# The tail of a two-layer decoder trunk on one core: the last 512 columns in two halves, the scaling ahead of the root, the last store on another queue

## The chip, the core and the metric

The kernel runs on one core of a Trainium2 chip. The core has five engines that run side by side, each with its own queue of instructions: TensorE (PE in the profile) multiplies matrices into PSUM, VectorE (DVE) and ScalarE (ACT) work elementwise on PSUM and SBUF, GpSimd (POOL) does little here, and SyncE (SP) issues most transfers. ACT can issue transfers too. PSUM has eight banks; a tile of 128 partitions by 512 float32 fills one. The metric is the device time of one execution in microseconds, lower is better.

## The reference

Two decoder layers on 256 tokens (16 learned tokens are put ahead and dropped at the end) with model width 1024. Each layer is a half-step SwiGLU block, a mixer (causal pooling in layer 0, differential attention in layer 1), and a second half-step SwiGLU block. Only the end of the last SwiGLU block matters here:

```python
def rmsnorm(x, g):
    xf = x.astype(jnp.float32)
    y = xf * lax.rsqrt(jnp.mean(xf * xf, axis=-1, keepdims=True) + EPS)
    return (y * g.astype(jnp.float32)).astype(x.dtype)

def swiglu(h, w1, w3, w2):
    return (jax.nn.silu(h @ w1) * (h @ w3)) @ w2
...
        f = swiglu(rmsnorm(h, ffn_norm_pre[i, 1]), ffn_w1[i, 1], ffn_w3[i, 1], ffn_w2[i, 1])
        h = h + 0.5 * rmsnorm(f, ffn_norm_post[i, 1])
    return h[:, N_META:]
```

So for each token: the 1024 columns of `f` are summed as squares, the inverse root of their mean scales them, the vector `ffn_norm_post` (the post-norm's) scales them by column, and half of that is added to `h`.

## The kernel before

Activations lie transposed (width on the partitions) until the last block's second projection, whose result has the tokens on the partitions. Every float32 product is three passes: each operand is split into a high and a low part, and `mm3` issues high x high, low x high and high x low into the same accumulation. Weights come in units of 128 x 1024 through SP's queue and are split by ACT (high) and DVE (low).

The order of the instructions on PE, ACT, DVE and SP is the order in which the code is written (`manual_schedule`); the framework only adds the waits on semaphores. A wait for another engine stands on the instruction that needs it, and everything behind that instruction on the same engine waits too.

`last_ffn` is the last SwiGLU block, without the 16 learned tokens. `ys[t][d]` are four PSUM banks: `t` is the block of 128 tokens, `d` the half of the 1024 output columns. `down(b)` adds the hidden block `b` to all four. The last three hidden blocks are kept back (`last`) and added bank by bank at the end, so that the banks become final one after the other: nine matmuls for each. When a bank is final,

- ACT squares it with `accum_out`, which leaves the sum over its columns in one column of `ms`;
- DVE makes `yg`, the bank times 0.5 times `gp` (the post-norm's vector, the same on all partitions);
- after the first bank DVE adds epsilon to the first sum (`part`); after the second, ACT takes the inverse root of the whole (`r`), DVE forms `v`, and with `q` and again `r` does one Newton step on the root;
- DVE makes `o`, `yg` times `r` plus `hn[t]` (the residual, transposed back earlier), in pieces of 512, 256 and 256 columns, and each piece is stored as soon as it is there. All stores are issued by SP but the middle one of the last token block, which ACT issues.

Of the kernel before, what the change touches and what calls it, by code (L numbers as in the profile page):

```python
# [9 lines left out]
F32 = mybir.dt.float32  # L10
F32R = mybir.dt.float32r
AF = mybir.ActivationFunctionType
ALU = mybir.AluOpType
# [3 lines left out]
P = 128  # L17
# [6 lines left out]
NB = FF // P  # L24
# [151 lines left out]
def trunk(ctx, tc, ht, w13a, w13b, w2t, w2n, wqkva, wqkv, wo, wp, lamv, mask, band, gpost, out):  # L176
    nc = tc.nc
# [68 lines left out]
    pfirst = const.tile([P, 2 * NK], F32, name="pfirst")  # L246
    pbg = const.tile([P, NK], F32, name="pbg")

    def mm3(out_ap, a, b, start, stop):

        nc.tensor.matmul(out_ap, lhsT=a[0], rhs=b[0], start=start, stop=False)  # L251
        nc.tensor.matmul(out_ap, lhsT=a[1], rhs=b[0], start=False, stop=False)  # L252
        nc.tensor.matmul(out_ap, lhsT=a[0], rhs=b[1], start=False, stop=stop)  # L253

    def wcol(parts, c, n=P):
        return parts[0][:, c:c + n], parts[1][:, c:c + n]

    def xcol(x, lo, hi):
        return x[0][:, lo:hi], x[1][:, lo:hi]
# [20 lines left out]
    def rsqrt(s, n, eps, tag, width=L, ahead=None):  # L280

        y = rsqrt_table(s, n, eps, tag, width)
        if ahead is not None:
            table(ahead, y[:, 0:1])
        newton(y, y, s, n, -0.5 * EPS if eps else 0.0)
        return y

    def table(func, src):

        nc.scalar.activation(out=dummy, in_=src, func=func)  # L290
# [218 lines left out]
    def first_blocks(res, us, spans, sums, refill, order):  # L509

        taken = []

        def go(k, pairs, start=False, stop=False):

            while len(taken) <= (6 * k + 5) // 8:
                taken.append(w.take())
            for a, x in pairs:
                for q, n in enumerate(spans):
                    u, c = divmod(6 * k + q, 8)
                    nc.tensor.matmul(us[q][:, :n], lhsT=taken[u][a][:, c * P:(c + 1) * P], rhs=x[:, :n],  # L520
                                     start=start, stop=stop)
                start = False

        res.lead = order[0]
        res.begin()
        ahead = sum(x is not None for x in res.hi)
        for k in range(ahead):
            go(k, [(0, res.hi[k]), (1, res.hi[k])], start=k == 0)
            if k == EXACT[res.n] and res.post.near:
                res.post.exact()  # L530
                res.refine()
        for i, k in enumerate(order):
            last = i == NK - 1
            res.tile(k, None if last else order[i + 1])
            hi, lo = res.x[k]
            if k >= ahead:
                go(k, [(0, hi)], start=k == 0)
                if last:
                    sums()
                go(k, [(1, hi)])  # L540
            elif last:
                sums()
            go(k, [(0, lo)], stop=last)
            left = 6 if last else 6 * min(order[i + 1:]) // 8
            w.refill(refill[i], held=max(SLACK, len(taken) - left))
# [570 lines left out]
    def last_ffn(res, fp, ubank, ybank, epsb):  # L1116
        n = SEQ

        us = [ubank() for _ in range(3)] + [ybank() for _ in range(3)]
        s2 = ybank()  # L1120

        def sums():
            nc.tensor.matmul(s2[:, :n], lhsT=ones, rhs=res.acc[:, :n], start=True, stop=True)
            for t in range(2):
                nc.tensor.matmul(s2[:, 300 + t:301 + t], lhsT=res.acc[:, t * P:(t + 1) * P], rhs=ones[:, 0:1],
                                 start=True, stop=True)

        first_blocks(res, us, [n] * 6, sums, REFILL, ORDER[4])
        r2 = rsqrt(s2[:, :n], n, True, "r2", ahead=AF.Silu)
        nc.vector.tensor_scalar(epsb, s2[:, 300:302], -0.5 * EPS, -2.0 * EPS, ALU.add, ALU.mult)  # L1130
        gate = Gate(n, r2, fp, False)
        gate.group(us)
        gate.paired = True
        gs = gate.parts
        gp = fp.tile([P, D], F32, name="gp")
        nc.sync.dma_start(out=gp, in_=gpost)
        hn = [fp.tile([P, D], F32, name=f"hn{t}", tag=f"hn{t}") for t in range(2)]

        def down(b):
            parts = w.take()  # L1140
            g = gs.pop(b)
            for t in range(2):
                for d in range(2):
                    mm3(ys[t][d], xcol(g, t * P, (t + 1) * P), wcol(parts, d * 512, 512), b == 0, b == NB - 1)

        for b in range(3, NB):
            u1, u3 = ubank(), ubank()
            for c, u in enumerate((u1, u3)):
                parts = w.take()
                for k in range(NK):  # L1150
                    nc.tensor.matmul(u, lhsT=parts[0][:, k * P:(k + 1) * P], rhs=res.pairs[k], start=k == 0, stop=k == NK - 1)  # L1151
                for k in range(NK):
                    nc.tensor.matmul(u[:, :n], lhsT=parts[1][:, k * P:(k + 1) * P], rhs=res.x[k][0], start=False,  # L1153
                                     stop=k == NK - 1, skip_group_check=True)
                if c == 0:
                    s = gate.silu(gate.scale(u1))
                    w.refill(2)
                else:
                    gate.product(b, s, u3)
                    w.refill(1)  # L1160
                    gate.low()
            if b == 3:
                ys = [[ybank(), ybank()] for _ in range(2)]
            down(b - 3)
            w.refill(1)
            if b in (8, 10, 12, 14):
                t, d = divmod((b - 8) // 2, 2)
                tr = ubank()
                for q in range(4):
                    nc.tensor.transpose(tr[:, q * P:(q + 1) * P], h[4 * d + q][:, t * P:(t + 1) * P], ident)  # L1170
                nc.scalar.copy(out=hn[t][:, d * 512:(d + 1) * 512], in_=tr)
        table(AF.Abs_reciprocal_sqrt, gate.s[:, 0:1])
        last = [(w.take(), gs.pop(b)) for b in range(NB - 3, NB)]
        for t in range(2):
            ms = fp.tile([P, 2], F32, tag="ms", name="ms", bufs=2)
            yg = fp.tile([P, D], F32, tag="yg", name="yg", bufs=2)
            junk = fp.tile([P, 512], F32, tag="junk", name="junk", bufs=1)
            o = fp.tile([P, D], F32, tag="o", name="o", bufs=2)
            for d in range(2):
                y = ys[t][d]  # L1180
                for q, (parts, g) in enumerate(last):
                    mm3(y, xcol(g, t * P, (t + 1) * P), wcol(parts, d * 512, 512), False, q == 2)
                nc.scalar.activation(out=junk, in_=y, func=AF.Square, scale=1.0 / 32.0, accum_out=ms[:, d:d + 1])
                if d == 0:
                    part = fp.tile([P, 1], F32, tag="part", name="part", bufs=2)
                    nc.vector.tensor_tensor(part, ms[:, 0:1], epsb[:, t:t + 1], ALU.add)
                else:
                    v = fp.tile([P, 1], F32, tag="v", name="v", bufs=2)
                    r = fp.tile([P, 1], F32, tag="r", name="r", bufs=2)
                    q = fp.tile([P, 1], F32, tag="q", name="q", bufs=2)  # L1190
                    nc.scalar.activation(out=r, in_=ms[:, 1:2], func=AF.Abs_reciprocal_sqrt, bias=part)
                    nc.vector.tensor_scalar(v, ms[:, 1:2], part, -0.5, ALU.add, ALU.mult)
                c = slice(d * 512, (d + 1) * 512)
                nc.vector.scalar_tensor_tensor(yg[:, c], y, 0.5, gp[:, c], ALU.mult, ALU.mult)
            nc.vector.scalar_tensor_tensor(q, r, r, v, ALU.mult, ALU.mult)
            nc.vector.scalar_tensor_tensor(r, q, 1.5, r, ALU.add, ALU.mult)
            for q, (c0, c1) in enumerate(((0, 512), (512, 768), (768, 1024))):
                nc.vector.scalar_tensor_tensor(o[:, c0:c1], yg[:, c0:c1], r, hn[t][:, c0:c1], ALU.mult, ALU.add)
                (nc.scalar if t and q == 1 else nc.sync).dma_start(out=out[t, :, c0:c1], in_=o[:, c0:c1])


    mp0, mp1 = C_MPOST, C_MPOST + NK
# [32 lines left out]
    with ExitStack() as stack:  # L1235
# [7 lines left out]
        with tc.tile_pool(name="ffn3", bufs=1, reuse_waits="tile") as fp:  # L1243

            epsb = fp.tile([P, 56], F32, name="epsb")[:, 0:2]
# [77 lines left out]
```

## Time and profile before

| what | value |
|---|---|
| median of 3 runs | 953.18 us (953.13 to 954.76) |
| the profiled execution | 953.05 us |
| its span, first to last instruction | 951.3 us |
| PE busy | 938.2 us (99%) |
| DVE, ACT busy | 636.8 us (67%), 502.4 us (53%) |
| mean granted TensorE clock | 0.998 of full speed |
| last matmul ends | at 944.53 us of the span |
| last store issued | at 948.08 us |

The span runs from the first to the last instruction; the time of the execution has 1.75 us more around it. Positions in the trace are microseconds from the start of the span. A matmul's start is recorded and its end modelled, and neighbouring matmuls overlap in the records, so the distance of two starts is what one costs. Rows of the timeline give start, duration, engine (PEld is the load of the stationary operand, SPq and ACTq are issues of transfers), line, operation, what is written <- what is read, shape, and in brackets the idle time before it with what ended it.

### The profile page before, as it was taken

To read this page: it belongs to the slowest core of one execution; us is meant where nothing else is said; L and a number is where in the kernel's file an instruction comes from. 1 tells how busy PE (TensorE), PEld (TensorE's weight loads), DVE (VectorE), ACT (ScalarE), POOL (GpSimd) and SP (SyncE) were. 2 spreads that over 40 slices of the span, in tenths; PEclk is the share of its full clock that TensorE was granted. 3 is DMA by queue.
4 is the path that set the end of the run, shared out by engine and by line. 5 is a ranking of instruction groups with operands and counts; after the bars stand their busy time and mean duration, and the time that the engine had idled before them with its cause. 6 is when DMAs were issued, how large, how long until landed. Compare 5 with 4: busy or idle time off the path is not lost.

```text
span 951.3 us, 17449 instructions
## 1 busy us (share of the span) xinstructions
PE 938.2 (99%) x6945; PEld 901.6 (95%) x6945; DVE 636.8 (67%) x1092; ACT 502.4 (53%) x865; POOL 15.4 (2%) x24
## 2 busy tenths in 40 slices
PE   9999999999999999999999999999999999999997
PEld 9999999998999999999999999999998998888885
DVE  7955554458975555448855554468877899777774
ACT  7744444435654445545744455446766756445432
POOL 0000000210000000000000000000001000000000
PEclk9999999999999999999999999999999999999999
DMA  9755557730475556551755556532523628655521
GB/s 318 266 197 177 168 156 220 221 117 1 143 257 176 170 155 199 176 190 45 265 179 178 166 172 188 186 99 91 177 95 121 206 89 294 215 190 184 180 89 44
DMA packets 48321, 160.74 MB, mean 169 GB/s; under 512 B 5360, under 2 KB 8944, under 8 KB 48240
## 3 DMA queue, kind: packets, MB, share of 16 engines
q1 hardware_dynamic: 47952, 159.31, 52.1%
q8 instruction: 54, 0.88, 0.4%
q10 hardware_dynamic: 288, 0.33, 0.1%
q14 instruction: 27, 0.22, 0.1%
HBM read 158.57 MB, written 1.05 MB: 168 GB/s over the span
## 4 chain that ended last, share of the span: by engine, by line
PE 95%; DVE 3%; ACT 1%; issue 1%; DMA 0%; DVEq 0%; ACTq 0%
PE bank L253 23%; PE bank L252 23%; PE bank L251 23%; PE bank L520 8%; PE bank L1151 7%; PE bank L1153 4%; PE bank L688 1%; DVE wlo L145 1%; PE bank L641 1%; PE bank L653 1%; PE bank L642 1%; DMA raw<-in_w13a 0%; ACT sc L875 0%; PE bank L852 0%; PE bank L843 0%
## 5 line engine op out<-in xcount | busy, mean ns | idle before, releaser
L145 DVE TENSOR_TENSOR wlo<-raw,whi 128x1024 fp32r<-128x1024 f32 (+1 forms) x296 | 353.7, 1198 | 58.5 <-PE bank L252 26.9
L133 ACT CAST whi<-raw 128x1024 fp32r<-128x1024 f32 (+1 forms) x296 | 299.8, 1029 | 50.7 <-PE bank L253 45.9
L251 PE MATMUL bank<-x,whi 128*128 128x272 f32 (+1 forms) x752 | 217.3, 289 | 0.0
L253 PE MATMUL bank<-x,whi 128*128 128x272 f32 (+1 forms) x752 | 216.8, 288 | 0.0
L252 PE MATMUL bank<-x,wlo 128*128 128x272 f32 (+1 forms) x752 | 215.7, 287 | 0.2 <-DVE wlo L145 0.2
L252 PEld LDWEIGHTS bank<-x,wlo 128*128 128x128 f32 x752 | 141.3, 188 | 0.5 <-DVE wlo L145 0.4
L251 PEld LDWEIGHTS bank<-x,whi 128*128 128x128 f32 x752 | 141.3, 188 | 0.5 <-issue 0.4
L253 PEld LDWEIGHTS bank<-x,whi 128*128 128x128 f32 x752 | 141.6, 188 | 0.0
L252 PE MATMUL bank<-ghi,wlo 128*128 128x272 f32 x484 | 140.0, 289 | 0.0
L251 PE MATMUL bank<-ghi,whi 128*128 128x272 f32 x484 | 140.0, 289 | 0.0
L253 PE MATMUL bank<-glo,whi 128*128 128x272 f32 x484 | 140.0, 289 | 0.0
L571 ACT ACTIVATE ua<-ua 128x272 f32<-128x272 f32 (+1 forms) x88 | 37.1, 429 | 142.6 <-DVE ua L557 142.6
L580 ACT CAST ghi<-ua 128x272 fp32r<-128x272 f32 (+1 forms) x88 | 36.1, 417 | 112.0 <-DVE ua L577 112.0
L251 PEld LDWEIGHTS bank<-ghi,whi 128*128 128x128 f32 x484 | 91.9, 190 | 0.0
L253 PEld LDWEIGHTS bank<-glo,whi 128*128 128x128 f32 x484 | 91.2, 188 | 0.0
L252 PEld LDWEIGHTS bank<-ghi,wlo 128*128 128x128 f32 x484 | 90.9, 188 | 0.0
L253 PE MATMUL bank<-xlo,whi 128*128 128x272 f32 x304 | 87.8, 289 | 0.0
L251 PE MATMUL bank<-xhi,whi 128*128 128x272 f32 x304 | 87.4, 287 | 0.0
L252 PE MATMUL bank<-xhi,wlo 128*128 128x272 f32 x304 | 87.3, 287 | 0.0
L577 DVE TENSOR_TENSOR ua<-bank,ua 128x272 f32<-128x272 f32 (+1 forms) x69 | 29.5, 438 | 71.4 <-PE bank L253 71.4
L1151 PE MATMUL bank<-xp,whi 128*128 128x512 f32 x304 | 76.1, 392 | 0.0
L1151 PEld LDWEIGHTS bank<-xp,whi 128*128 128x128 f32 x304 | 55.5, 188 | 10.5
(243 smaller groups left out, 1371.4 us busy)
## 6 DMA issues: line engine op xcount, KB each, us to landing
raw<-in_w13b SPq DMA_DIRECT2D x152, 512.0 KB, 4.2
raw<-in_w2t SPq DMA_DIRECT2D x48, 448.0 KB, 3.4
raw<-in_w2t SPq DMA_DIRECT2D x24, 512.0 KB, 3.6
raw<-in_w2n SPq DMA_DIRECT2D x22, 512.0 KB, 3.7
raw<-in_w13a SPq DMA_DIRECT2D x18, 512.0 KB, 4.3
raw<-in_wqkv SPq DMA_DIRECT2D x18, 512.0 KB, 4.2
raw<-in_wo SPq DMA_DIRECT2D x8, 512.0 KB, 3.7
raw<-in_wqkva SPq DMA_DIRECT2D x6, 512.0 KB, 4.2
```

The lines of the kernel that those rows point to most:

```text
L133: self.nc.scalar.copy(out=hi[:, :n], in_=self.raws[u][:, :n])
L145: self.nc.vector.tensor_tensor(lo[:, :n], raw[:, :n], hi[:, :n].bitcast(F32), ALU.subtract)
L251: nc.tensor.matmul(out_ap, lhsT=a[0], rhs=b[0], start=start, stop=False)
L252: nc.tensor.matmul(out_ap, lhsT=a[1], rhs=b[0], start=False, stop=False)
L253: nc.tensor.matmul(out_ap, lhsT=a[0], rhs=b[1], start=False, stop=stop)
L520: nc.tensor.matmul(us[q][:, :n], lhsT=taken[u][a][:, c * P:(c + 1) * P], rhs=x[:, :n], start=start, stop=stop)
L571: nc.scalar.activation(out=a[:, :self.n], in_=a[:, :self.n], func=AF.Silu)
L577: nc.vector.tensor_tensor(s[:, :n], self.sum(u3), s[:, :n], ALU.mult)
L580: nc.scalar.copy(out=hi, in_=s[:, :n])
L641: nc.tensor.matmul(y[:, :n], lhsT=a[0], rhs=x[0], start=b == 0, stop=False)
L1151: nc.tensor.matmul(u, lhsT=parts[0][:, k * P:(k + 1) * P], rhs=res.pairs[k], start=k == 0, stop=k == NK - 1)
L1153: nc.tensor.matmul(u[:, :n], lhsT=parts[1][:, k * P:(k + 1) * P], rhs=res.x[k][0], start=False, stop=k == NK - 1, skip_group_check=True)
```

## The change

For the last token block (`t` = 1) the second bank is no longer accumulated by nine matmuls of 512 columns. Nine matmuls make its columns 0 to 255 final, then nine its columns 256 to 511; both halves stay in the one bank. Each half has its own Square, its own column of `ms` and its own `yg`. The first token block keeps two pieces of 512.

For both token blocks `yg` now stands ahead of `part`, and the last `yg` ahead of `v`, `q` and `r` (the small tiles are all named `n` now: `part`, `v`, `r` and `q2`). The last store of the last token block is issued by ACT and the middle one by SP, the other way round than before.

The new argument `part` of `mm3` and the place of `stop` in `down` only set flags of the accumulation groups.

```diff
--- before.py
+++ after.py
@@ -246,11 +246,11 @@
     pfirst = const.tile([P, 2 * NK], F32, name="pfirst")
     pbg = const.tile([P, NK], F32, name="pbg")
 
-    def mm3(out_ap, a, b, start, stop):
-
-        nc.tensor.matmul(out_ap, lhsT=a[0], rhs=b[0], start=start, stop=False)
-        nc.tensor.matmul(out_ap, lhsT=a[1], rhs=b[0], start=False, stop=False)
-        nc.tensor.matmul(out_ap, lhsT=a[0], rhs=b[1], start=False, stop=stop)
+    def mm3(out_ap, a, b, start, stop, part=False):
+
+        nc.tensor.matmul(out_ap, lhsT=a[0], rhs=b[0], start=start, stop=False, skip_group_check=part)
+        nc.tensor.matmul(out_ap, lhsT=a[1], rhs=b[0], start=False, stop=False, skip_group_check=part)
+        nc.tensor.matmul(out_ap, lhsT=a[0], rhs=b[1], start=False, stop=stop, skip_group_check=part)
 
     def wcol(parts, c, n=P):
         return parts[0][:, c:c + n], parts[1][:, c:c + n]
@@ -1141,7 +1141,7 @@
             g = gs.pop(b)
             for t in range(2):
                 for d in range(2):
-                    mm3(ys[t][d], xcol(g, t * P, (t + 1) * P), wcol(parts, d * 512, 512), b == 0, b == NB - 1)
+                    mm3(ys[t][d], xcol(g, t * P, (t + 1) * P), wcol(parts, d * 512, 512), b == 0, b == NB - 4 and t == d == 1)
 
         for b in range(3, NB):
             u1, u3 = ubank(), ubank()
@@ -1172,31 +1172,31 @@
         table(AF.Abs_reciprocal_sqrt, gate.s[:, 0:1])
         last = [(w.take(), gs.pop(b)) for b in range(NB - 3, NB)]
         for t in range(2):
-            ms = fp.tile([P, 2], F32, tag="ms", name="ms", bufs=2)
+
+            cuts = (0, 512, 768, 1024) if t else (0, 512, 1024)
+            m = len(cuts) - 1
+            ms = fp.tile([P, m], F32, tag=f"ms{t}", name="ms")
             yg = fp.tile([P, D], F32, tag="yg", name="yg", bufs=2)
             junk = fp.tile([P, 512], F32, tag="junk", name="junk", bufs=1)
             o = fp.tile([P, D], F32, tag="o", name="o", bufs=2)
-            for d in range(2):
-                y = ys[t][d]
+            part, v, r, q2 = [fp.tile([P, 1], F32, tag=f"n{i}", name="n", bufs=2) for i in range(4)]
+            for i in range(m):
+                c = slice(cuts[i], cuts[i + 1])
+                n = cuts[i + 1] - cuts[i]
+                y = ys[t][cuts[i] // 512][:, cuts[i] % 512:cuts[i] % 512 + n]
                 for q, (parts, g) in enumerate(last):
-                    mm3(y, xcol(g, t * P, (t + 1) * P), wcol(parts, d * 512, 512), False, q == 2)
-                nc.scalar.activation(out=junk, in_=y, func=AF.Square, scale=1.0 / 32.0, accum_out=ms[:, d:d + 1])
-                if d == 0:
-                    part = fp.tile([P, 1], F32, tag="part", name="part", bufs=2)
-                    nc.vector.tensor_tensor(part, ms[:, 0:1], epsb[:, t:t + 1], ALU.add)
-                else:
-                    v = fp.tile([P, 1], F32, tag="v", name="v", bufs=2)
-                    r = fp.tile([P, 1], F32, tag="r", name="r", bufs=2)
-                    q = fp.tile([P, 1], F32, tag="q", name="q", bufs=2)
-                    nc.scalar.activation(out=r, in_=ms[:, 1:2], func=AF.Abs_reciprocal_sqrt, bias=part)
-                    nc.vector.tensor_scalar(v, ms[:, 1:2], part, -0.5, ALU.add, ALU.mult)
-                c = slice(d * 512, (d + 1) * 512)
+                    mm3(y, xcol(g, t * P, (t + 1) * P), wcol(parts, cuts[i], n), False, q == 2, n < 512)
+                nc.scalar.activation(out=junk[:, :n], in_=y, func=AF.Square, scale=1.0 / 32.0, accum_out=ms[:, i:i + 1])
                 nc.vector.scalar_tensor_tensor(yg[:, c], y, 0.5, gp[:, c], ALU.mult, ALU.mult)
-            nc.vector.scalar_tensor_tensor(q, r, r, v, ALU.mult, ALU.mult)
-            nc.vector.scalar_tensor_tensor(r, q, 1.5, r, ALU.add, ALU.mult)
+                if i < m - 1:
+                    nc.vector.tensor_tensor(part, ms[:, i:i + 1], part if i else epsb[:, t:t + 1], ALU.add)
+            nc.scalar.activation(out=r, in_=ms[:, m - 1:m], func=AF.Abs_reciprocal_sqrt, bias=part)
+            nc.vector.tensor_scalar(v, ms[:, m - 1:m], part, -0.5, ALU.add, ALU.mult)
+            nc.vector.scalar_tensor_tensor(q2, r, r, v, ALU.mult, ALU.mult)
+            nc.vector.scalar_tensor_tensor(r, q2, 1.5, r, ALU.add, ALU.mult)
             for q, (c0, c1) in enumerate(((0, 512), (512, 768), (768, 1024))):
                 nc.vector.scalar_tensor_tensor(o[:, c0:c1], yg[:, c0:c1], r, hn[t][:, c0:c1], ALU.mult, ALU.add)
-                (nc.scalar if t and q == 1 else nc.sync).dma_start(out=out[t, :, c0:c1], in_=o[:, c0:c1])
+                (nc.scalar if t and q == 2 else nc.sync).dma_start(out=out[t, :, c0:c1], in_=o[:, c0:c1])
 
 
     mp0, mp1 = C_MPOST, C_MPOST + NK
```

How it stands on the engines at the end of the program, with the waits. On PE, the end before (bank_9757 is `ys[1][1]`; `whi`, `wlo` are the weights' parts, `ghi`, `glo` the hidden block's):

```order
L253 MATMUL bank_9756<-wlo_11069,ghi_11126 128x512
L251 MATMUL bank_9757<-whi_10999,ghi_10996 128x512
L252 MATMUL bank_9757<-whi_10999,glo_10997 128x512
...
L252 MATMUL bank_9757<-whi_11043,glo_11127 128x512
L253 MATMUL bank_9757<-wlo_11069,ghi_11126 128x512
```

and now, around the seam between the halves:

```order
L253 MATMUL bank_9756<-wlo_11069,ghi_11126 128x512
L251 MATMUL bank_9757<-whi_10999,ghi_10996 128x256
...
L252 MATMUL bank_9757<-whi_11043,glo_11127 128x256
L253 MATMUL bank_9757<-wlo_11069,ghi_11126 128x256
L251 MATMUL bank_9757<-whi_10999,ghi_10996 128x256 [waits DVE_49]
L252 MATMUL bank_9757<-whi_10999,glo_10997 128x256
```

Nine matmuls became eighteen into the same bank, and the first of the second half waits for a count of DVE's that is reached by `yg` of the first half.

On DVE, the last token block before (bank_9756 is `ys[1][0]`):

```order
L1186 TENSOR_TENSOR part_11198<-ms_11184,epsb_9368 128x1 [waits Activation_49]
L1194 SCALAR_TENSOR_TENSOR yg_11185<-bank_9756,gp_9686 128x512
L1192 TENSOR_SCALAR v_11211<-ms_11184,part_11198 128x1 [waits DVE_49,Activation_49]
L1194 SCALAR_TENSOR_TENSOR yg_11185<-bank_9757,gp_9686 128x512
L1195 SCALAR_TENSOR_TENSOR q_11213<-r_11212,v_11211 128x1 [waits DVE_49,Activation_49]
L1196 SCALAR_TENSOR_TENSOR r_11212<-q_11213,r_11212 128x1 [waits DVE_49]
```

and now (n_11188 is `part`, n_11189 `v`, n_11190 `r`, n_11191 `q2`):

```order
L1190 SCALAR_TENSOR_TENSOR yg_11185<-bank_9756,gp_9686 128x512 [waits Activation_49]
L1192 TENSOR_TENSOR n_11188<-ms_11184,epsb_9368 128x1
L1190 SCALAR_TENSOR_TENSOR yg_11185<-bank_9757,gp_9686 128x256 [waits Activation_49]
L1192 TENSOR_TENSOR n_11188<-ms_11184,n_11188 128x1 [waits DVE_49]
L1190 SCALAR_TENSOR_TENSOR yg_11185<-bank_9757,gp_9686 128x256 [waits Activation_49]
L1194 TENSOR_SCALAR n_11189<-ms_11184,n_11188 128x1 [waits DVE_49]
L1195 SCALAR_TENSOR_TENSOR n_11191<-n_11190,n_11189 128x1 [waits DVE_49,Activation_49]
L1196 SCALAR_TENSOR_TENSOR n_11190<-n_11191,n_11190 128x1 [waits DVE_49]
```

The last `yg` moved ahead of `v`, each `yg` waits for the Square of the same bank, and one `yg` and one `part` are new.

On ACT, the last token block before:

```order
L1183 ACTIVATE junk_11186,ms_11184<-bank_9756 128x512 [waits PE_49]
L1183 ACTIVATE junk_11186,ms_11184<-bank_9757 128x512 [waits PE_49,Activation_49]
L1191 ACTIVATE r_11212<-ms_11184,part_11198 128x1 [waits DVE_49,Activation_49]
L1199 DMA out_0<-o_11187 128x256 [waits DVE_49]
L1318 UNCONDITIONAL_BRANCH
```

and now:

```order
L1189 ACTIVATE junk_11186,ms_11184<-bank_9756 128x512 [waits PE_49]
L1189 ACTIVATE junk_11186,ms_11184<-bank_9757 128x256 [waits PE_49,Activation_49]
L1189 ACTIVATE junk_11186,ms_11184<-bank_9757 128x256 [waits DVE_49,PE_49]
L1193 ACTIVATE n_11190<-ms_11184,n_11188 128x1 [waits DVE_49,Activation_49]
L1199 DMA out_0<-o_11187 128x256 [waits DVE_49]
```

The Square of the second half waits for DVE as well as for PE. The store at the end is the middle piece before, the last piece now.

## The prediction

> **What bounds the kernel now.** I read the page's first part, then the chain that ended last for the final microseconds, then the timeline of the same stretch.
>
> ```profile
> span 951.3 us, 17449 instructions
> PE 938.2 (99%) x6945; PEld 901.6 (95%) x6945; DVE 636.8 (67%) x1092; ACT 502.4 (53%) x865; POOL 15.4 (2%) x24
> ```
>
> TensorE is busy 99% of the span, so the whole kernel is bound by matmuls; the change leaves all of them but the last nine alone. What it can move is the tail behind them. The chain there (start, length, what):
>
> ```profile
> 944.29 0.24 PE bank L253
> ...
> 944.62 0.07 ACT junk L1183
> ...
> 945.11 0.20 ACT junk L1183
> ...
> 945.34 0.21 DVE v L1192
> ...
> 945.61 0.46 issue
> 946.07 0.22 DVE q L1195
> ...
> 946.31 0.17 DVE r L1196
> ...
> 946.50 0.75 DVE o L1198
> 947.26 0.40 DVEq L1318
> 947.65 0.40 DVE o L1198
> ```
>
> The last matmul ends at 944.53, and 6.8 us remain to 951.3: sum of squares on ACT (0.7 us), root and Newton step (1.2), three products on DVE (1.55), then the last store. Even a perfect overlap could touch only the first two, and 0.2% of 953.18 us, about what a measurement of this kernel can tell from no change, is 1.91 us.
>
> The timeline rows of the tail (start, duration):
>
> ```profile
> 941.39 0.68 DVE L1194 SCALAR_TENSOR_TENSOR yg<-bank,gp 128x512 f32<-128x512 f32 x1
> 941.99 0.21 DVE L1195 SCALAR_TENSOR_TENSOR q<-r,v 128x1 f32<-128x1 f32 x1
> 942.32 0.39 PE L251 MATMUL bank<-whi,ghi 128*128 128x512 f32 x1
> 942.43 1.54 DVE L1198 SCALAR_TENSOR_TENSOR o<-yg,r,hn 128x512 f32<-128x512 f32 x3
> 943.01 0.19 ACT L1183 ACTIVATION_READ_ACCUMULATOR junk<-bank 128x1 f32 x1
> 943.89 0.15 DVE L1186 TENSOR_TENSOR part<-ms,epsb 128x1 f32<-128x1 f32 x1
> 943.96 0.68 DVE L1194 SCALAR_TENSOR_TENSOR yg<-bank,gp 128x512 f32<-128x512 f32 x1
> 944.13 0.39 PE L253 MATMUL bank<-wlo,ghi 128*128 128x512 f32 x1
> 944.62 0.60 ACT L1183 ACTIVATE junk<-bank 128x512 f32<-128x512 f32 x1 [1.41 <-PE bank L253]
> 945.34 0.29 ACT L1191 ACTIVATE r<-ms,part 128x1 f32<-128x1 f32 x1
> 945.47 0.68 DVE L1194 SCALAR_TENSOR_TENSOR yg<-bank,gp 128x512 f32<-128x512 f32 x1
> ```
>
> See three things. The nine matmuls that the change halves start at 942.32 and the ninth at 944.13, (944.13 - 942.32) / 8 = 0.226 us apart, without a gap. DVE is occupied with the first token block's products until 942.43 + 1.54 = 943.97, so it is late for the second block: the accumulator of that block's first 512 columns was read at 943.01 + 0.19 = 943.20, yet `part` came at 943.89. And `r` was ready at 945.34 + 0.29 = 945.63, yet `q` started at 946.07, because `yg` (started 945.47) stood between; one `yg` keeps DVE 941.99 - 941.39 = 0.60 us.
>
> **The change, part by part.**
>
> *The halves.* Nine matmuls of 512 columns become nine on columns 512-767 and nine on columns 768-1023, both in one PSUM bank. In the built program the tenth of them waits for a DVE count, and ACT's Square of the second half waits for DVE too: these stand in the order shown with the change. That count is reached by `yg` of the first half, which itself waits for the first half's Square. So PE stops after nine, until ACT and then DVE have read the first half. Before, nothing stood between. Behind the waiting matmul on PE are only the other eight; waiting for them are Square, `yg`, the root and all that follows.
>
> Where the trace shows PE write a bank while another engine reads it, there would be a row for what overlap costs; it shows none, since each bank is read after its ninth matmul.
> The Trainium skill, page "PSUM — Partial Sum Buffer", section "PSUM bank collisions raise a hardware error", says that any two of TensorE, ScalarE and VectorE collide when they access one bank on the same partitions at once, disjoint columns and two readers included, and that guards go by bank, not by address. By that rule the wait cannot be removed while both halves share a bank, and the sum is the loss below; by dependences on columns alone it would be the small gain of the first rival. No run here shows a collision.
>
> Prices for 256 columns, from the attention block:
>
> ```profile
> 755.66 0.39 ACT L449 ACTIVATE sq<-bank 128x256 f32<-128x256 f32 x1
> 729.40 0.42 DVE L272 SCALAR_TENSOR_TENSOR nt<-bank,nt 128x256 f32<-128x256 f32 x1
> 730.40 0.48 DVE L932 SCALAR_TENSOR_TENSOR of<-bank,subg,oy 128x256 f32<-128x256 f32 x1
> 729.61 0.39 PE L251 MATMUL bank<-ohi,whi 128*128 128x256 f32 x1 [0.84 <-ACT am L902]
> 729.84 0.28 PE L252 MATMUL bank<-ohi,wlo 128*128 128x256 f32 x1
> 730.53 0.28 PE L252 MATMUL bank<-ohi,wlo 128*128 128x256 f32 x1
> ```
>
> Matmuls of 256 columns follow each other at (730.53 - 729.84) / 6 = 0.115 us (six steps between these two rows), and the first after a wait needs 0.23 until the second. A Square of 256 takes 0.39 against 0.60, 0.21 less. A `yg` of 256 takes 0.42 to 0.48; I take 0.42, whose row has the same kind of operands (a bank and a full tile), 0.26 less than 0.68, so it keeps DVE 0.34.
>
> What a restart of PE after DVE costs, from the longest such wait of the trace:
>
> ```profile
> 228.22 0.44 DVE L310 TENSOR_TENSOR x<-a,rt 128x272 fp32r<-128x272 f32 x1
> 228.78 0.80 PEld L520 LDWEIGHTS bank<-x,whi 128*128 128x128 f32 x6 [2.09 <-issue]
> 228.81 1.00 PE L520 MATMUL bank<-x,whi 128*128 128x272 f32 x6 [1.69 <-DVE x L310]
> ```
>
> DVE ended at 228.66, PE started at 228.81: 0.15 us.
>
> *Scaling ahead of the root.* `yg` now stands before `v` on DVE. In the first token block this makes `v` and `q` later: `yg` starts at about 941.26, `v` at 941.86, `q` at 941.86 + 0.21 + 0.02 = 942.09 instead of 941.99, so the three products end at 944.07 instead of 943.97. That 0.10 us is passed on, since DVE is the late one in the next block.
>
> The second block, step by step:
> - First half, PE: 942.32 + 8 x 0.115 = 943.24, last one ends at +0.28 = 943.52. Square starts 0.1 later (944.62 against 944.53 before), at 943.62, its sum is read by about 944.1.
> - DVE: `yg` of the first 512 columns starts at 943.97 + 0.10 - 0.08 (`part` began 0.08 before the products' end) = 943.99; `part` 0.60 later, 944.59; `yg` of the first half 0.07 later (943.96 - 943.89), 944.66, and ends at 945.08. Here DVE, not ACT, is last.
> - PE restarts at 945.08 + 0.15 = 945.23, after 945.23 - 943.52 = 1.7 us of standing still. The ninth starts 0.23 + 7 x 0.115 = 1.04 later and ends at 946.27 + 0.28 = 946.55. Before it was 944.53: 2.0 us later.
> - Square of the second half at 946.64. From Square to the first instruction that uses its sum were 945.34 - 944.62 = 0.72; less 0.21 is 0.51: 947.15. `yg` 0.34, `v` 0.21 + 0.02, then `q` at 947.72. Before, that stretch was 946.07 - 945.34 = 0.73, now 0.57: the move ahead of the root and the shorter half together give 0.16 back, the shorter Square 0.21.
> - `q` to `o` as before (946.50 - 946.07 = 0.43): the products start at 948.15 instead of 946.50, 1.65 us later.
>
> *The last store.* The middle store goes from ACT's queue to SP's, the last from SP's to ACT's.
>
> ```profile
> 947.69 0.36 ACTq L1199 DMA_DIRECT2D out<-o  x1
> 948.08 0.33 SPq L1199 DMA_DIRECT2D out<-o  x1
> ...
> out<-o ACTq DMA_DIRECT2D x1, 128.0 KB, 2.2
> out<-o SPq DMA_DIRECT2D x1, 128.0 KB, 2.3
> ```
>
> (The last two rows are of the answer on transfers: queue, KB, us to landing.) DVE's last product ended at 948.05 and SP issued 0.03 later: SP had been free, so no wait is taken away. SP gets the middle store one issue (0.33) after its first, which is done before the product is ready. Landing took 2.2 on ACT's queue and 2.3 on SP's: worth -0.1 to 0, and between the ends I take -0.05, as the two transfers also share what they move with. The range keeps 0.15 either way.
>
> *The rest* (flags of the matmul groups, names of the small tiles, one more `part` of 0.15 us beside PE's standstill) adds nothing to the path; the instructions ahead are the same. If that `part` lost its cover, it would cost 0.15.
>
> Sum: +1.65 - 0.05 = +1.6 us. The profiled execution (953.05 us, span 951.3, 1.75 around it) becomes 954.65; it stood 0.13 under the median of the runs, so the forecast is 953.18 + 1.6 = **954.8 us**, +0.17%: a loss, but inside what counts as no change.
>
> **Rivals.**
> 1. *The halves do overlap*: PE goes on at 943.47 as if the wait were met. For it: ACT is idle and could take the first half. Against it: the wait in the built order, and DVE's backlog. Then PE ends at 944.55 as before, and the 0.21 and 0.16 are won: -0.4 with the store, 952.8 us, still no change. Nothing in 6.8 us of tail gives the 1.91 for "faster".
> 2. *The clock falls during the standstill* (slower by more than 0.2%). The granted clock (next-to-last columns: PEclk, DMA share, GB/s):
>
> ```profile
> 227.00:229.00 2.00, 0.31 (x2) 0.22 (x2) 1.90 (x5) 1.75 (x4) 0.00 (x0) 1.00 0.00 0
> ...
> 947.00:947.50 0.50, 0.00 (x0) 0.00 (x0) 0.50 (x2) 0.00 (x0) 0.00 (x0) 0.72 0.00 0
> 947.50:948.00 0.50, 0.00 (x0) 0.00 (x0) 0.50 (x2) 0.00 (x0) 0.00 (x0) 0.50 0.00 0
> ```
>
> After the last matmul the clock halves: 0.72 over half a microsecond, at 1.0 and 0.5, puts the step at 947.22, 2.7 us after 944.53. Against the rival: 1.69 us without a matmul at 227-229 left it at 1.00, and 1.7 is what I expect now. For it: one sample of each. Nine matmuls at half the rate cost about 1.0 to 1.3 more, 955.9 us; a fall with three of the nine to come (+0.3) is the point from which it decides.
> The Trainium skill, page "TensorE: Matmul & The Clock Gate", section "What's actually happening", has the gate judge free-running windows of about 3.4 us; by that, half a window of standstill should not close it, but where the window lies varies from run to run.
>
> **How the numbers follow.** The waiting case has 0.80, with a range of its own of 954.3 to 955.3: `yg` at 0.48 adds 0.1 twice, the store 0.15, the restart and the two hand-overs of ACT some 0.1 each, and as much below. About a fifth of it lies over 955.09, the bound for "slower". Rival 1 has 0.07, rival 2 0.10, anything else 0.03. So slower 0.16 + 0.10 + 0.01 = 0.27, faster 0.02, same 0.71. The range runs from 953.9 (a restart much cheaper than the row, runs scattering by a few tenths) to 955.9 (rival 2); rival 1 stays outside below.
>
> **What the changed profile would show.** PE idle once, 1.7 us, from about 943.5, put down to `yg` on DVE; `yg` of the first half starting 0.5 us after its Square's sum was there, behind `part`; last matmul ending near 946.5 with PEclk still 1.00; `q` 0.57 us behind the second half's sum; the last store issued by ACT near 949.7. Wrong would be: no gap on PE (rival 1), matmuls 0.23 us apart after it (rival 2), or `yg` of the first half starting at 944.1, ahead of DVE's backlog (a loss of only 1.1).

## The result, and the profile after

The changed kernel takes 954.71 us (median of 18 runs, 954.49 to 956.25), the kernel before in the same rounds 953.18 us (18 runs): a ratio of 1.0015, with a 95% interval of 1.0009 to 1.0022. That is a loss of 1.5 us, clear of the scatter, and under the 0.2% that the prediction drew as its line; 954.8 us were forecast. In the rounds of the experiments two executions lay far off the others (1013.54 us of the kernel before, 3265.23 us of the kernel with a standstill of 3.05 us); the intervals leave them out, and without them the medians shown move by at most 0.06 us.

The profiled execution took 955.0 us. Its first part on the page:

```profile
span 953.2 us, 17470 instructions
PE 938.9 (99%) x6954; PEld 902.7 (95%) x6954; DVE 637.1 (67%) x1094; ACT 502.4 (53%) x867; POOL 15.7 (2%) x24
```

PE has nine matmuls and 0.7 us of busy time more, ACT and DVE two instructions each. None of that is 1.5 us; it is in the waits. PE's waits in the last 15 us (engine, what it waited for, total us, times, longest):

```profile
PEld bank L251 <- DVE yg L1190: 1.9, 1, 1.9
PE bank L251 <- DVE yg L1190: 1.7, 1, 1.7
```

PE waited once for DVE, which it never did in this stretch before. The timeline around that wait:

```profile
942.65 0.28 PE L251 MATMUL bank<-whi,ghi 128*128 128x256 f32 x1
942.96 1.54 DVE L1198 SCALAR_TENSOR_TENSOR o<-yg,n,hn 128x512 f32<-128x512 f32 x3
943.60 0.28 PE L253 MATMUL bank<-wlo,ghi 128*128 128x256 f32 x1
943.97 0.38 ACT L1189 ACTIVATE junk<-bank 128x256 f32<-128x256 f32 x1 [0.44 <-PE bank L253]
944.25 0.20 ACT L1189 ACTIVATION_READ_ACCUMULATOR junk<-bank 128x1 f32 x1
944.42 0.68 DVE L1190 SCALAR_TENSOR_TENSOR yg<-bank,gp 128x512 f32<-128x512 f32 x1
945.02 0.15 DVE L1192 TENSOR_TENSOR n<-ms,epsb 128x1 f32<-128x1 f32 x1
945.09 0.42 DVE L1190 SCALAR_TENSOR_TENSOR yg<-bank,gp 128x256 f32<-128x256 f32 x1
945.56 0.39 PE L251 MATMUL bank<-whi,ghi 128*128 128x256 f32 x1 [1.68 <-DVE yg L1190]
945.78 0.28 PE L252 MATMUL bank<-whi,glo 128*128 128x256 f32 x1
946.61 0.28 PE L253 MATMUL bank<-wlo,ghi 128*128 128x256 f32 x1
```

See first the gap: the ninth matmul of the first half ends at 943.60 + 0.28 = 943.88, the tenth starts at 945.56. Then who is late: the sum of the first half's squares was there at 944.45, but DVE did the first block's products until 944.50, then `yg` of 512 columns, then `part`, and came to `yg` of the first half only at 945.09. That one ends at 945.51, and PE goes on 0.05 us later.

The chain after the last matmul, to set against the one of before:

```profile
946.93 0.03 ACT junk L1189
...
947.21 0.20 ACT junk L1189
...
947.43 0.42 DVE yg L1190
947.86 0.13 DVE n L1194
947.99 0.03 issue
948.02 0.02 DVEq L1195
948.04 0.06 issue
948.10 0.23 DVE n L1195
...
948.35 0.17 DVE n L1196
...
948.54 0.75 DVE o L1198
```

From Square to `yg` are 947.43 - 946.93 = 0.50 us (0.72 from Square to `v` before). From there to `q` (L1195) are 0.67 us, against 0.73 before. To compare the two profiles, count from the first of the split matmuls (942.32 before, 942.65 after; the 0.33 between them arose ahead of the change): the products start 4.18 us behind it before, 5.89 us after. That is +1.71.

### The profile page after: what moved, and what is told of

It reads as the page before. It is cut to its first block, busy times and chain, and to the rows that moved or that the text cites. A ratio compares the mean times of both kernels' runs of the same rounds, so it can differ in the third digit from the quotient of the medians.

```text
span 953.2 us, 17470 instructions
## 1 busy us (share of the span) xinstructions
PE 938.9 (99%) x6954; PEld 902.7 (95%) x6954; DVE 637.1 (67%) x1094; ACT 502.4 (53%) x867; POOL 15.7 (2%) x24
## 4 chain that ended last, share of the span: by engine, by line
PE 94%; DVE 3%; ACT 1%; issue 1%; DMA 0%; DVEq 0%; ACTq 0%
PE bank L253 23%; PE bank L252 23%; PE bank L251 23%; PE bank L520 8%; PE bank L1151 7%; PE bank L1153 4%; PE bank L688 1%; DVE wlo L145 1%; PE bank L641 1%; PE bank L653 1%; PE bank L642 1%; DMA raw<-in_w13a 0%; ACT sc L875 0%; PE bank L852 0%; PE bank L843 0%
```

## The experiments

The kernels were timed in three groups, each in five rounds beside the kernel before on one chip, another chip for each group. Differences are of medians in the same rounds, each uncertain by about 0.8 us by the stated intervals (1.1 and 1.3 us for the two longer standstills), though most runs of one kernel lie within 0.8 us. So the profile decides what the times alone cannot. Theory A is the prediction's: PE stands still since both halves share a bank, for as long as DVE needs to read the first half.

**The halves alone** (`yg` behind `part` and `v`, the stores as before):

```diff
                 nc.scalar.activation(out=junk[:, :n], in_=y, func=AF.Square, ...)
-                nc.vector.scalar_tensor_tensor(yg[:, c], y, 0.5, gp[:, c], ALU.mult, ALU.mult)
                 if i < m - 1:
                     nc.vector.tensor_tensor(part, ...)
-            nc.scalar.activation(out=r, ...)
-            nc.vector.tensor_scalar(v, ...)
+                else:
+                    nc.scalar.activation(out=r, ...)
+                    nc.vector.tensor_scalar(v, ...)
+                nc.vector.scalar_tensor_tensor(yg[:, c], y, 0.5, gp[:, c], ALU.mult, ALU.mult)
...
-                (nc.scalar if t and q == 2 else nc.sync).dma_start(...)
+                (nc.scalar if t and q == 1 else nc.sync).dma_start(...)
```

> The halves alone, with yg behind part and v as before, and the stores on their old queues. Theory A (PE stands still between the halves because they share a bank): PE idles about 1.7 us again; v goes ahead of the last yg, so from the second half's sum to q only about 0.47 us pass instead of the 0.67 of the changed kernel, the first block's products end 0.1 us earlier, and the last store is 0.1 us dearer: about 1.3 us over the kernel before, 954.5 us. Rival B (the order of yg is what costs): within 0.3 us of the kernel before.

954.18 us against 953.01: +1.17 us (ratio 1.0012, 1.0004 to 1.0021). From its timeline:

```profile
945.09 0.39 PE L251 MATMUL bank<-whi,ghi 128*128 128x256 f32 x1 [1.54 <-DVE yg L1195]
947.01 0.21 DVE L1194 TENSOR_SCALAR n<-ms,n 128x1 f32<-128x1 f32 x1 [1.98 <-ACT junk L1189]
947.14 0.41 DVE L1195 SCALAR_TENSOR_TENSOR yg<-bank,gp 128x256 f32<-128x256 f32 x1
947.48 0.21 DVE L1196 SCALAR_TENSOR_TENSOR n<-n 128x1 f32<-128x1 f32 x1
```

The gap is there without the new order, 0.14 us shorter since DVE came free earlier, and from `v` to `q` pass 0.47 us, as expected. The halves carry most of the loss, and rival B falls.

**Order and stores alone** (no halves):

```diff
-                    mm3(ys[t][d], ..., b == 0, b == NB - 4 and t == d == 1)
+                    mm3(ys[t][d], ..., b == 0, b == NB - 1)
...
-            cuts = (0, 512, 768, 1024) if t else (0, 512, 1024)
+            cuts = (0, 512, 1024)
```

> No halves: the second block's last bank is accumulated by nine matmuls of 512 columns again; yg ahead of part and of v, and the exchanged stores stay. Theory A: no gap on PE; yg of 512 (0.60 us of DVE) and then v (0.33 until q) stand between the sum and q, 0.93 us against 0.73 before, so q is 0.2 us later and the store 0.1 to 0.15 us cheaper: 0.0 to +0.1 us against before, 953.2 to 953.3 us. Rival B: it carries the loss, +1.0 us or more.

953.18 against 953.01: +0.17 us (1.0001, 0.9992 to 1.0010), no gap on PE.

```profile
945.33 0.69 DVE L1190 SCALAR_TENSOR_TENSOR yg<-bank,gp 128x512 f32<-128x512 f32 x1 [0.49 <-ACT junk L1189]
945.94 0.20 DVE L1194 TENSOR_SCALAR n<-ms,n 128x1 f32<-128x1 f32 x1
946.26 0.22 DVE L1195 SCALAR_TENSOR_TENSOR n<-n 128x1 f32<-128x1 f32 x1
```

From the sum to `q` are 0.93 us, against 0.73 in the old order: with `yg` ahead, `v` and its hand-over to `q` no longer hide behind `yg`. By the profile the new order costs 0.2 us; the times cannot tell it from nothing.

**The second half in a bank of its own.** Every instruction of the changed kernel stays; for columns 768 to 1023 of the last 128 tokens the sums of the earlier hidden blocks are left out.

```diff
+                if i == 2:
+                    y = ubank()[:, :n]
                 for q, (parts, g) in enumerate(last):
-                    mm3(y, ..., False, q == 2, n < 512)
+                    mm3(y, ..., i == 2 and q == 0, q == 2, n < 512 and i == 1)
```

> The changed kernel with the second half (columns 768 to 1023 of the last 128 tokens) accumulated in a bank of its own that nobody reads; the sums of the earlier hidden blocks for these columns are left out. Every instruction of the changed kernel is still there, in the same order. Theory A: no wait on PE, the eighteen matmuls follow each other at 0.12 us, the last ends about 0.1 us later than the ninth did before; the products start 0.2 us earlier than before and the store is 0.1 us cheaper: -0.3 us, 952.9 us. Rival C (the loss comes from twice the matmuls, the third Square and the extra small instructions): +1.0 us or more, as in the changed kernel.

952.89 against 953.01: -0.12 us (0.9998, 0.9989 to 1.0007).

```profile
943.59 0.28 PE L253 MATMUL bank<-wlo,ghi 128*128 128x256 f32 x1
943.61 0.38 ACT L1191 ACTIVATE junk<-bank 128x256 f32<-128x256 f32 x1 [0.44 <-PE bank L253]
943.71 0.28 PE L251 MATMUL bank<-whi,ghi 128*128 128x256 f32 x1
...
945.58 0.29 ACT L1195 ACTIVATE n<-ms,n 128x1 f32<-128x1 f32 x1 [0.42 <-DVE n L1194]
```

The tenth matmul follows the ninth by 0.12 us, while ACT reads the first half. So the loss is the wait, and the wait comes from the shared bank; twice the matmuls, a third Square and a second `part` cost little (rival C falls): the last matmul ends 944.59 - 942.28 = 2.31 us behind the first split one, 0.10 later than the 944.53 - 942.32 = 2.21 of before. A bank is one tile in this program, so the runs do not tell whether the waits are set by bank or by tile. Of the 0.3 us expected as a gain the times show 0.1, less than they can tell from nothing. The last row shows a new delay: ACT's root starts 0.42 us after the sum was read. The row puts it down to DVE's second `part`, but that ran from 945.05 to 945.20 and the sum was read until 945.16; what filled most of the 0.42 us the profile does not show.

**No backlog on DVE.** The first block's products go behind the first half's `yg` of the second block.

```diff
+        held = []
...
+                if i == 1 and held:
+                    held.pop()()
...
-            for q, (c0, c1) in enumerate(((0, 512), (512, 768), (768, 1024))):
+            def products(t=t, o=o, yg=yg, r=r):
+                for q, (c0, c1) in enumerate(((0, 512), (512, 768), (768, 1024))):
...
+            if t:
+                products()
+            else:
+                held.append(products)
```

> The changed kernel with the first token block's three products (1.55 us of DVE) and their stores moved behind the first half's yg and part of the second block. Theory A (in the standstill DVE is late, not ACT): yg of the first half starts as soon as its Square's sum is there and DVE has done the yg of 512, about 0.6 us earlier; PE stands still about 1.1 us instead of 1.7; the products that were moved run beside PE's second half. About 0.6 us under the changed kernel: +1.0 us against before, 954.1 us. Rival D (ACT's Square sets the length of the standstill): no change against the changed kernel, 954.7 us, or worse if the moved products end after the second half's sum.

954.16 against 953.01: +1.15 us (1.0011, 1.0002 to 1.0020), where the changed kernel has +1.53 in its own rounds.

```profile
944.27 0.42 DVE L1191 SCALAR_TENSOR_TENSOR yg<-bank,gp 128x256 f32<-128x256 f32 x1 [0.16 <-ACT junk L1190]
944.75 0.39 PE L251 MATMUL bank<-whi,ghi 128*128 128x256 f32 x1 [1.08 <-DVE yg L1191]
```

Now `yg` waits for ACT, and the gap is 1.08 us instead of 1.68. The times differ by 0.4 us, less than they can tell apart, but in the profile the last products start 947.72 - 942.43 = 5.29 us behind the first split matmul instead of 5.89. DVE's backlog was 0.6 us of the standstill, as expected, and rival D falls. What stays is ACT's reading and then DVE's.

**Only ACT reads between the halves** (`yg` once, 512 columns, behind the second half):

```diff
+                if n == 512 or i == 2:
+                    if i == 2:
+                        c = slice(512, 1024)
+                        y = ys[t][1]
                     nc.vector.scalar_tensor_tensor(yg[:, c], y, 0.5, gp[:, c], ALU.mult, ALU.mult)
```

> The changed kernel, but DVE reads the bank only once, behind the second half (one yg of 512 columns, as before the change): between the halves only ACT's Square reads it. Theory A (any reader of the bank holds PE): PE waits for ACT instead of DVE, from the end of the first half to the sum about 0.6 us and a restart, 0.7 us of standstill instead of 1.7; the last matmul 1.0 us later than before; yg of 512 and v then stand between sum and q, 0.93 us; with the store +0.8 us against before, 953.8 us. Rival E (only DVE's reading or DVE's count holds PE): no gap, -0.1 us or less.

953.88 against 953.18: +0.70 us (1.0007, 0.9998 to 1.0016).

```profile
943.86 0.38 PE L251 MATMUL bank<-whi,ghi 128*128 128x256 f32 x1 [0.62 <-ACT junk L1189]
```

PE is held by ACT's reading too, 0.62 us; rival E falls. Even this shortest reading costs more by the profile than the smaller Square gives back: the last matmul ends 945.20 - 942.01 = 3.19 us behind the first split one, 0.98 later than before, and the Square gives back 0.21. The times alone do not show the loss; their interval reaches no change.

**A longer standstill**, to see when the clock falls. The first half's `yg` is made four times, then seven times:

```diff
-                nc.vector.scalar_tensor_tensor(yg[:, c], y, 0.5, gp[:, c], ALU.mult, ALU.mult)
+                for _ in range(4 if n < 512 and i == 1 else 1):
+                    nc.vector.scalar_tensor_tensor(yg[:, c], y, 0.5, gp[:, c], ALU.mult, ALU.mult)
```

> The changed kernel with the first half's yg made four times instead of once (the same result each time), so that PE's standstill grows by three times 0.34 us to about 2.7 us. If the clock holds through it: the changed kernel plus 1.0 us, +2.6 us against before, in every run. If the clock rival is only a matter of length: in the runs in which the granted clock falls during the gap or behind it, matmuls of the second half are 0.23 us apart instead of 0.12, and those runs are up to 1.0 us longer still (+3.6 us); since the place of the drop relative to the last matmul differed from profile to profile (0.65 to 5 us), the times would fall into groups.

956.25 against 953.18: +3.07 us (1.0030, 1.0019 to 1.0042), all runs but the one of 3265.23 us within 955.95 to 956.40.

```profile
946.94 0.39 PE L251 MATMUL bank<-whi,ghi 128*128 128x256 f32 x1 [3.05 <-DVE yg L1191]
947.16 0.28 PE L252 MATMUL bank<-whi,glo 128*128 128x256 f32 x1
947.28 0.28 PE L253 MATMUL bank<-wlo,ghi 128*128 128x256 f32 x1
```

The gap grew to 3.05 us, not 2.7: repetitions into the same tile follow each other by 0.456 us. Against the changed kernel that is 3.07 - 1.53 = 1.54 us more for a gap that is 1.37 us longer, no more than the scatter apart; matmuls are 0.12 us apart behind the gap, and no group of runs a microsecond longer appears.

Seven times:

> The changed kernel with the first half's yg made seven times, so that PE's standstill is about 1.7 + 6 x 0.456 = 4.4 us (one repetition cost 0.456 us in the run with three of them). If the clock does not fall in a gap of this length: +1.37 us against the run with three repetitions, +4.4 us against before, in every run. Clock rival: after the last matmul the clock fell after 0.45 to 5 us in the profiles so far, so in most runs it now falls inside the gap or the second half: matmuls 0.23 us apart there, up to 1.0 us more, and times spread over a microsecond.

958.52 against 953.11: +5.4 us (1.0056, 1.0042 to 1.0070), all runs within 958.31 to 958.57.

```profile
948.33 0.39 PE L251 MATMUL bank<-whi,ghi 128*128 128x256 f32 x1 [4.43 <-DVE yg L1191]
948.55 0.35 PE L252 MATMUL bank<-whi,glo 128*128 128x256 f32 x1
948.70 0.41 PE L253 MATMUL bank<-wlo,ghi 128*128 128x256 f32 x1
948.91 0.42 PE L251 MATMUL bank<-whi,ghi 128*128 128x256 f32 x1
949.13 0.42 PE L252 MATMUL bank<-whi,glo 128*128 128x256 f32 x1
```

Its granted clock (third column from the right):

```profile
948.25:948.50 0.25, 0.17 (x1) 0.17 (x2) 0.09 (x2) 0.00 (x0) 0.00 (x0) 1.00 0.00 0
948.50:948.75 0.25, 0.25 (x3) 0.25 (x4) 0.00 (x0) 0.00 (x0) 0.00 (x0) 0.74 0.00 0
948.75:949.00 0.25, 0.25 (x3) 0.25 (x3) 0.00 (x0) 0.00 (x0) 0.00 (x0) 0.50 0.00 0
```

After 4.43 us the clock halves at 948.62, 0.3 us into the second half, and matmuls go from 0.12 to 0.21 us apart. From PE's restart to the last products are 952.10 - 948.33 = 3.77 us, against 949.98 - 946.94 = 3.04 with the 3.05 us gap: 0.73 us is the price of the slower clock. The times agree within their scatter: 5.41 - 3.07 = 2.34 us, of which the longer gap explains 1.38. So rival 2 exists, but it did not show at 1.7 us.

**The exchange of the stores alone**, and the kernel before once more:

```diff
-                (nc.scalar if t and q == 1 else nc.sync).dma_start(out=out[t, :, c0:c1], in_=o[:, c0:c1])
+                (nc.scalar if t and q == 2 else nc.sync).dma_start(out=out[t, :, c0:c1], in_=o[:, c0:c1])
```

> The kernel before with the stores exchanged alone: the middle one of the last block on SP's queue, the last on ACT's. From the profiles so far: from the start of the products to the end of the span 4.66 us with the exchange, 4.80 without: -0.14 us, 952.9 us, below what the times can tell apart, but to be read in the profile. Rival: the 0.14 is scatter of one profile, then nothing.

> The kernel before once more, for its profile alone: from the start of the last three products to the end of the span. If the exchange of the stores is worth something, it is 4.75 us or more as in the first profile (4.80); if that was scatter, about 4.6 us, as in the run with the halves alone, whose stores stayed on their old queues (4.59).

The exchange alone takes 952.95 us against 953.18: -0.23 us (0.9996, 0.9988 to 1.0005). From the start of the products to the end of the span were 4.80 and 4.83 us (946.07 to 950.9) in the two profiles of the kernel before, but 4.59 (947.91 to 952.5) with the halves alone, which has the old stores too; with the exchange 4.56 to 4.68 in all profiles. The last store landed 2.3 us after its issue in both profiles of the kernel before, 2.1 with the halves alone and 2.1 on ACT's queue, so the difference lies in the landing. It may be worth 0.15 us; with one of three old profiles on the other side and times that cannot resolve it, this stays open.

**A whole kernel with the second half in its own bank**: the earlier blocks' sums are split into two parts (one cast on ACT, one subtraction on DVE) and carried over by two matmuls with the identity; order of `yg` as before, stores exchanged.

```diff
+        own = ubank()[:, :256]
...
+        nc.scalar.copy(out=chi, in_=ys[1][1][:, 256:512])
+        nc.vector.tensor_tensor(clo, ys[1][1][:, 256:512], chi.bitcast(F32), ALU.subtract)
...
+                if t and i == 0:
+                    nc.tensor.matmul(own, lhsT=ident_r, rhs=chi, start=True, stop=False)
+                    nc.tensor.matmul(own, lhsT=ident_r, rhs=clo, start=False, stop=False)
...
```

> A whole kernel built on the own-bank run: the second half of the last bank gets a bank of its own, and the earlier blocks' sums for it are split into two parts (one cast on ACT, one subtraction on DVE, both while these engines idle) and carried over by two matmuls with the identity, 0.24 us of PE; yg behind part and v as before the change, stores exchanged. Theory A: no gap on PE, last matmul 0.35 us later than before, from there to q 0.6 us shorter (0.21 Square, 0.26 yg, and r is ready when yg is done), store 0.14 cheaper: about -0.3 us, 952.7 us. Rival: the two matmuls or their waits disturb PE, then no gain.

952.89 against 953.18: -0.29 us (0.9998, 0.9989 to 1.0007).

```profile
938.51 0.60 ACT L1200 ACTIVATE junk<-bank 128x512 f32<-128x512 f32 x1 [1.29 <-PE bank L253]
...
946.54 1.54 DVE L1210 SCALAR_TENSOR_TENSOR o<-yg,n,hn 128x512 f32<-128x512 f32 x3
```

There is no gap, but from the first Square of the tail to the last block's products are 8.03 us, against 946.50 - 938.44 = 8.06 before. The two extra matmuls take back what the halves give: the first split matmul starts 4.14 us behind that Square instead of 3.88, and from there to the products are 3.89 us instead of 4.18. And what is left of the time is no more than the exchange of the stores showed alone. No version was found that is measurably better than the kernel before.

## Why the prediction was right, point by point

Counted from the first split matmul, in us:

| step | forecast | profile after |
|---|---|---|
| first half's last matmul ends | 1.20 | 1.23 |
| PE stands still | 1.71 | 1.68 |
| first half's `yg` starts | 2.34 | 2.44 |
| PE goes on | 2.91 | 2.91 |
| last matmul ends | 4.23 | 4.24 |
| from the second half's sum to `q` | 0.57 | 0.67 |
| products start | 5.83 | 5.89 |

In the profile before, the products start at 4.18.

- *The wait and its length.* Right, with its cause: the own-bank run takes it away, the run without the backlog shortens it to 1.08, as the listed order of DVE's work said. Two terms were mis-sized by 0.1 us each, and that they cancelled is luck. `yg` came 0.1 later, because `v` to `q` in the first block took 942.51 - 942.19 = 0.32 us instead of the 0.23 assumed; the restart took 0.05 us (945.51 to 945.56) instead of 0.15.
- *`yg` ahead of the root.* The 0.16 us expected to come back here were 0.06, by the same term. In the chain after, between `v` and `q` stand two stretches of issue and a semaphore instruction of DVE's queue (L1195): `q` waits for DVE's own `v` and for ACT, two counts. Before, `v` was long done when `q` came. That the two counts cost the 0.1 us was not tried alone. The order alone costs 0.2 us in the profile of its own run.
- *The store.* -0.05 was taken, 4.80 - 4.66 = 0.14 appeared in the profile; open, as said above, and inside the range kept for it.
- *Rival 1* (the halves overlap) did not occur in the change, and its price was too good by about 0.3 us. Its sum was 0.1 us off: with PE going on at 943.47, the last matmul would end near 944.67, not 944.55. In the own-bank run the products start 946.36 - 942.28 = 4.08 us behind the first split matmul, 0.10 under the 4.18 of before, where the Square and the order together were to give 0.37. Two pieces of the difference can be read off: 0.1 between `v` and `q`, and 0.1 because the eighteen matmuls end later; `q` also waited for the late root, which cost it less than 0.1.
- *Rival 2* (the clock falls) did not occur in the profile: PEclk is 1.00 through the second half. Of the 18 runs 17 lie within 954.49 to 955.00; the other, 956.25, shows no fall by itself, as two runs of the kernel before (954.76 and 955.07) are as far out without a gap. The price of 1.0 to 1.3 us was somewhat high beside the 0.73 us that the 4.43 us gap showed, where the clock fell 0.3 us into the second half.
- *The sum.* +1.6 forecast, +1.53 measured; the profile alone gives 1.71 - 0.14 = 1.57. The interval of the measured difference is 0.9 to 2.1 us, so that the times agree to 0.1 is in part luck; the steps of the profile are what bears the mechanism out.

```profile
945.20:946.50 1.30, 0.94 (x8) 0.94 (x9) 0.37 (x2) 0.00 (x0) 0.00 (x0) 1.00 0.65 224
948.50:948.75 0.25, 0.00 (x0) 0.00 (x0) 0.21 (x2) 0.00 (x0) 0.00 (x0) 0.93 0.00 0
948.75:949.00 0.25, 0.00 (x0) 0.00 (x0) 0.25 (x1) 0.00 (x0) 0.00 (x0) 0.50 0.00 0
```

These rows of the changed kernel show the clock at 1.00 while the second half ran, and its fall at 948.71, 1.8 us after the last matmul.

The Trainium skill, page "PSUM — Partial Sum Buffer", section "PSUM bank collisions raise a hardware error", has PSUM guarded by bank, in its simple form, and not by address; the program's waits agree with it, and their price here is 1.68 us of standstill with DVE's backlog, 1.08 without it, 0.62 with ACT as the only reader. That the hardware would have collided without the wait was not tried.

## What to carry to other kernels

In this program, cutting an accumulation in two so that its reading can overlap worked only with the halves in different PSUM banks; in one bank the second half waits for every reader of the first, and the wait ends with the last of them. Even with two banks nothing measurable was won here (952.89 against 953.18 us). Before splitting, look up what the reader's engine still has to do at that moment: here DVE's older products, not the reading itself, were the last third of the gap (0.6 of 1.68 us). And an instruction that fills another engine's waiting time (`yg` behind `v`, during the root) is better not moved ahead of what that engine's result will be combined with; here that cost 0.2 us by the profile.

## What the runs showed of the hardware

- A gap on PE does not slow it at once. Behind 1.68 and 3.05 us the matmuls of the profiles kept their 0.12 us; behind 4.43 us they went to 0.21 us apart, and all five times agree with that. This says little of longer work behind a gap: the second half lasts only 1.3 us, and the clock fell 0.4 us after its end with the gap of 3.05 us, 0.65 us with the gap of 1.54 us (halves alone).
- The fall is not a fixed time after PE stops. In the six profiles without a gap it came 2.0 to 5.0 us after the last matmul (2.7 in the first of the kernel before, 5.0 in the own-bank run). In the six with a gap it came 3.5 to 4.8 us after the gap began, whatever ran behind the gap. The Trainium skill, page "TensorE: Matmul & The Clock Gate", section "What's actually happening", describes free-running windows of about 3.4 us. By that, the fall would lie elsewhere in the span from run to run, and the spread agrees; how busy a window must be was not measured. In the three kernels with gaps of 1.68, 3.05 and 4.43 us it came at 948.71, 948.70 and 948.62 us of the span, in the other nine profiles between 946.9 and 949.6; the three equal instants may be chance.
- In the changed kernel the first matmul of 256 columns after the wait is followed by the second after 0.22 us, the others follow after 0.12.
- Repeating one DVE instruction into the same tile takes 0.456 us each, where different tiles' neighbours (`yg` of 256 columns to `v`) follow after 0.34. Why was not looked into.
